# Delta-rule recurrence of a hybrid decoder layer: priority for its VectorE and ScalarE steps, and named places for its small products

## The chip, the cores and the metric

The kernel runs on one core of one Trainium2 chip. The metric is the device time of one execution in microseconds; the median of three runs of the kernel before is 2295.15 us (2294.39 to 2297.28).

## What is computed

Two layers of a parallel-branch decoder trunk with 512 tokens and a model width of 1024, in float32. Each layer normalises its input, projects it, runs three branches (a Mamba-2 scan, latent attention, a gated delta rule), merges them by sigmoid gates, projects the merge, and adds an MLP. The change lies in the gated delta rule. Cut to that, the reference is:

```python
def gated_delta_chunked(q, k, v, g, beta):      # L = 64 tokens a chunk
    ...
    a_mat = jnp.where(strict, einsum(kb, k) * decay, 0.0)
    rhs = concatenate([v * beta, kb * exp(g)])
    u, w = split(triangular_solve(a_mat + eye, rhs))
    qk = where(incl, einsum(q, k) * decay, 0.0)

    def step(state, inp):
        v_new = uc - wc @ state
        o = (qc * exp(gc)) @ state + ac @ v_new
        state = state * exp(g_last) + (kc * exp(g_last - gc)).T @ v_new
        return state, o

def gdn_mixer(...):
    ...
    o = rmsnorm(gated_delta_chunked(q, k, v, g, beta), norm_g) * silu(z)

mixed = g_ssd * (y_ssd @ w_ssd_out) + g_mla * (y_mla @ w_mla_out) + g_gdn * (y_gdn @ w_gdn_out)
```

## The kernel before, in words

**Dense products.** Each float32 operand is split into a rounded high part and the rest (`split_half`, L172 on ScalarE and L173 on VectorE, both with priority for weights), and a product is three matmuls of 128 x 128 by 512 (`mm3`, L200 to L202). `dense_F` (the weights stationary) forms two output tiles of 128 columns from eight k tiles: 48 matmuls, ordered by pairs of k tiles and within them by output tile `j`. It takes a `tag`; after the last matmul of k tile `kk` for output `j`, it calls `place((tag, kk, j), ...)`. The weights of a pair of k tiles need one of four buffers, and raw weights come through two. There are four PSUM banks for dense products (`acc`), three for small ones (`sm`), one for others (`yt`).

**The order.** The program is written tile by tile; a scheduler, run when the program is built, decides each engine's instruction order by priority and by its own model of durations, and adds semaphores. On the chip each engine runs its list in order. `tc.high_priority()` puts the instructions inside it ahead of others that are ready. `behind(key, ins)` asks that `ins` come after the matmul that `place` records under `key`, in TensorE's list alone: it adds no semaphore. Before the change it is used in the Mamba branch and in `gdn_matrix`.

**The delta rule.** Eight value heads are worked as two units (`gdn_unit`, `u` = 0 and 1) of four heads, two key heads each, in four steps `t` of 128 tokens. `gdn_matrix` and `gdn_inverse` have made the inverse `Y` of the triangular system ahead. A unit first does its dense products: the query tiles (`key_tiles`, tag `(ly, "k", 2u)`), the values (two `dense_F`), and the gate `z` (`silu_T`). Then come the four steps; the scheduler lays them among the dense products that follow in the program: those of unit 1 for unit 0, and the output projection's for unit 1 (`out_proj`: for each pair `dp` of output tiles a gate product, tag `(ly, 2, dp, "g")`, and a `y` product, tag `(ly, 2, dp, "y")`, whose k tiles 0 to 3 are unit 0's results and 4 to 7 unit 1's). One step holds:

- `pg` (L1039, TensorE): keys by queries; `gk` (L1041) and `pt_` (L1043) on VectorE mask and scale it; the decays `e` come by DMA.
- `pk` (L1048): keys by state; four VectorE instructions (L1050), one a head, subtract it from the values: `r`.
- `pw` (L1053): `Y` by `r`, one matmul a head, each seen in the trace as two instructions.
- `vn` (L1055, VectorE) and `vd` (four at L1060, ScalarE) scale `pw`.
- `pS` (L1063) and four VectorE instructions (L1069) make the next state. It closes the loop: the next step's `pk` waits for it.
- `po` (L1072) and, for t > 0, `pq` (L1077) give the output; ScalarE copies `po` (L1078), VectorE adds `pq` (L1080).
- The closing norm: squares (L1086, ScalarE), small VectorE instructions (L1090 to L1095) with a power on GpSimd in their midst (L278), and the gate, four at L1098.

After the four steps the gated tiles are transposed by columns `c` (L1103, four a column, in the one `yt` bank) and split into `yh` and `yl` (L273 on ScalarE, L274 on VectorE). The values' and keys' causal convolution (`gconv_silu`, L719 and three L723 a tile) has priority on both engines already.

Of the kernel before, what the change touches and what calls it, by code (L numbers as in the profile page):

```python
# [14 lines left out]
AF = mybir.ActivationFunctionType  # L15
# [5 lines left out]
P = 128  # L21
S = 512
T = S // P
# [32 lines left out]
def hybrid_kernel(ctx, tc, a, out, depth=2, taps=None):  # L56
# [4 lines left out]
    def mk(pl, shape, dt, tag, bufs=None):  # L61
        return pl.tile(shape, dt, tag=tag, name=f"{tag}_{next(uid)}", bufs=bufs)
# [120 lines left out]
    def weights(w2d, c0, n, K, hold=None, raw0=None):  # L183

        kt = min(1024 // n, K // P)
        step = 512 // n
        for k0 in range(0, K // P, kt):  # L190
            given = raw0 is not None and k0 == 0
            raw = raw0 if given else weights_raw(w2d, c0, n, k0, kt)
            for q in range(0, kt, step):
                hi, lo = split_half(raw[:, q * n : (q + step) * n], hold and hold[k0 + q], not given)
                v = lambda x: x.rearrange("p (k n) -> p k n", n=n)
                yield k0 + q, v(hi), v(lo)
# [37 lines left out]
    def tiles(n):  # L234
        return [slice(i, i + P) for i in range(0, n, P)]
# [147 lines left out]
    for ly in range(depth):  # L383
# [612 lines left out]
        def gdn_unit(u, kT, ork, cc, cd, Yt, yh, yl):  # L996
            hd0 = 16 + 4 * u
            qT = key_tiles(2 * u, between)
            pss = sm_bank()
            for i in range(2):  # L1000
                sq = mk(br, [P, S], F32, "ft4", 2)
                act.activation(sq, qT[i], AF.Square)
                for t in range(T):
                    pe.matmul(pss[:, i * T + t : i * T + t + 1], sq[:, t * P : (t + 1) * P], ones[:, 0:1], start=True, stop=True)
            ssq = mk(sp, [P, 2, T], F32, "gss", 2)
            dve.tensor_scalar(ssq.rearrange("p i t -> p (i t)"), pss[:, :8], 4.0 * EPS, None, ALU.add)
            rq = mk(sp, [P, 2, T], F32, "grq", 2)
            pool.tensor_tensor(rq.rearrange("p i t -> p (i t)"), ssq.rearrange("p i t -> p (i t)"), nhalf[:, :8], ALU.pow)
            ktok = [mk(br, [P, T, P], F32, "kt", 2) for i in range(2)]
            for i in range(2):  # L1010
                ps = sm_bank()
                for t in range(T):
                    pe.transpose(ps[:, t * P : (t + 1) * P], kT[i][:, t * P : (t + 1) * P], ident)
                act.copy(ktok[i].rearrange("p t n -> p (t n)"), ps)
            v = mk(br, [P, T, 512], F32, "tok", 5)
            gz = mk(br, [P, T, 512], F32, "tok", 5)
            for i in range(2):
                for j, pj in enumerate(dense_F(weights(w_in, O_GV + (4 * u + 2 * i) * P, 256, D), tiles(256), D, xh, xl)):
                    h = 2 * i + j
                    vf = mk(br, [P, S], F32, "ft4", 2)  # L1020
                    gconv_silu(pj, 8 + 4 * u + h, vf)
                    ps = sm_bank()
                    for t in range(T):
                        pe.transpose(ps[:, t * P : (t + 1) * P], vf[:, t * P : (t + 1) * P], ident)
                    dve.tensor_tensor(v[:, :, h * P : (h + 1) * P], ps.rearrange("p (t n) -> p t n", t=T),
                                      bc_last(ork[:, i, :], P), ALU.mult)
            silu_T(br, O_GZ + 512 * u, gz)

            hdec = lambda i, t, h: dec[:, i, t, hd0 + h : hd0 + h + 1]
            ss = mk(sp, [P, T, 4], F32, "gos", 2)  # L1030
            st = None
            for t in range(T):
                tok = slice(t * P, (t + 1) * P)
                Y = Yt[:, t]
                e = mk(br, [P, 4, P], F32, "eE", 4)
                sync.dma_start(e, d_e[u, t])
                pg = sm_bank()
                for i in range(2):
                    pe.matmul(pg[:, i * P : (i + 1) * P], kT[i][:, tok], qT[i][:, tok], start=True, stop=True)  # L1039
                gk = mk(br, [P, 2, P], F32, "gk", 2)  # L1040
                dve.tensor_tensor(gk, hv(pg)[:, 0:2], bc_mid(incl, 2), ALU.mult)  # L1041
                pt_ = e
                dve.tensor_tensor(prs(pt_), prs(e), bc_j(gk), ALU.mult)  # L1043
                r = v[:, t, :]
                if t > 0:
                    pk = sm_bank()
                    for i in range(2):
                        pe.matmul(pk[:, i * 256 : (i + 1) * 256], kT[i][:, tok], st[:, i * 256 : (i + 1) * 256], start=True, stop=True)  # L1048
                    for h in range(4):
                        dve.scalar_tensor_tensor(hv(r)[:, h], hv(pk)[:, h], ndec[:, t, 4 * u + h : 4 * u + h + 1], hv(r)[:, h], ALU.mult, ALU.add)  # L1050
                pw = sm_bank()
                for h in range(4):
                    pe.matmul(pw[:, h * P : (h + 1) * P], Y[:, h, :], r[:, h * P : (h + 1) * P], start=True, stop=True)  # L1053
                vn = mk(br, [P, 512], F32, "wk1")
                dve.tensor_tensor(hv(vn), hv(pw), bc_last(cc[:, t, :], P), ALU.mult)  # L1055
                sn = None
                if t < T - 1:
                    vd = mk(br, [P, 512], F32, "wk2")
                    for h in range(4):
                        act.activation(hv(vd)[:, h], hv(pw)[:, h], AF.Copy, scale=cd[:, t, h : h + 1])  # L1060
                    pS = sm_bank()
                    for i in range(2):
                        pe.matmul(pS[:, i * 256 : (i + 1) * 256], ktok[i][:, t, :], vd[:, i * 256 : (i + 1) * 256], start=True, stop=True)  # L1063
                    sn = mk(br, [P, 512], F32, "st", 2)
                    if t == 0:
                        act.copy(sn, pS)
                    else:
                        for h in range(4):
                            dve.scalar_tensor_tensor(hv(sn)[:, h], hv(st)[:, h], hdec(2, t, h), hv(pS)[:, h], ALU.mult, ALU.add)  # L1069
                po = sm_bank()  # L1070
                for h in range(4):
                    pe.matmul(po[:, h * P : (h + 1) * P], pt_[:, h, :], vn[:, h * P : (h + 1) * P], start=True, stop=True)  # L1072
                o = mk(br, [P, 512], F32, "wk3")
                if t > 0:
                    pq = sm_bank()
                    for i in range(2):
                        pe.matmul(pq[:, i * 256 : (i + 1) * 256], qT[i][:, tok], st[:, i * 256 : (i + 1) * 256], start=True, stop=True)  # L1077
                    act.copy(o, po)  # L1078
                    for h in range(4):
                        dve.scalar_tensor_tensor(hv(o)[:, h], hv(pq)[:, h], hdec(0, t, h), hv(o)[:, h], ALU.mult, ALU.add)  # L1080
                else:
                    act.copy(o, po)
                st = sn
                for h in range(4):
                    jk = mk(br, [P, P], F32, "gk", 2)
                    act.activation(jk, o[:, h * P : (h + 1) * P], AF.Square, accum_out=ss[:, t, h : h + 1])  # L1086

                rqt = mk(sp, [P, 4], F32, "grt", 2)
                for j in range(2):
                    dve.tensor_scalar(rqt.rearrange("p (i j) -> p i j", j=2)[:, :, j], rq[:, :, t], 128.0 ** -0.5, None, ALU.mult)  # L1090
                ms = mk(sp, [P, 4], F32, "gms", 2)
                dve.tensor_tensor(ms, ss[:, t, :], rqt, ALU.mult)
                dve.tensor_tensor(ms, ms, rqt, ALU.mult)
                rsq(ms, ms, 1.0 / 128, EPS)
                dve.scalar_tensor_tensor(ms, ms, 0.5, rqt, ALU.mult, ALU.mult)  # L1095
                for h in range(4):
                    gzh = hv(gz[:, t, :])[:, h]
                    dve.scalar_tensor_tensor(gzh, gzh, ms[:, h : h + 1], hv(o)[:, h], ALU.mult, ALU.mult)  # L1098
            for c in range(4):
                k = 4 * u + c  # L1100
                ps = y_bank()
                for t in range(T):
                    pe.transpose(ps[:, t * P : (t + 1) * P], gz[:, t, c * P : (c + 1) * P], ident)  # L1103
                split_gain(yh[k], yl[k], ps, col(g_gdn))
                tap(f"ygdn{k}", f32(yh[k]))

# [337 lines left out]
```

## Time and profile before

| | |
|---|---|
| median of 3 runs | 2295.15 us |
| profiled execution, its own time | 2296.46 us |
| its span | 2294.7 us |
| memory read and written over the span | 103 GB/s |
| dense matmul over a 512-wide tile, modelled duration | about 0.39 us |
| weight casts L172 over 512 columns | 536 from `wraw`, 620 ns each |
| weight rests L173 over 512 columns | 536 from `wraw`, 686 ns each |

The span is what the hardware profiler saw of the program between its first and last instruction; the profiled execution's own time is a little longer. Views give start and duration in microseconds, the engine, the source line, the operation, the tiles written and read, and how many like instructions follow each other; in brackets stands how long the engine had been idle and what ended the wait. PE is TensorE, PEld its weight load, DVE VectorE, ACT ScalarE, POOL GpSimd. Ends of matmuls are modelled, so what one costs in a stream is read from start to start. In the table of windows a row has the stretch and its length, then each engine's busy time and instructions (PE, PEld, DVE, ACT, POOL), the granted clock, the DMA share and GB/s. In the list of waits a row has the waiting line, what it waited for, the total in microseconds, the number of waits, and the longest.

### The profile page before, as it was taken

The page shows a single profiled execution, that of the slowest core. Times are in us where ns is not written, and L with a number is a line of the kernel's source. Part 1 is how long each engine was busy: PE and PEld are TensorE (multiplying, and loading weights), DVE is VectorE, ACT ScalarE, POOL GpSimd, SP SyncE. Part 2 cuts the span into 40 slices and gives each one's busy share as a digit, 9 for nine tenths or more (in the row PEclk, how much of TensorE's full clock was granted, in tenths as well). Part 3 has the DMA queues.
Part 4 walks back from the last instruction along what each step waited for, and adds up shares of the span by engine and source line. Part 5 has one row for each costly group of instructions (what it writes and reads, how often), then busy time and mean ns, then how long its engine had stood idle before and what let it go on. Part 6 is the DMA issues. An engine that isn't in the chain of part 4 may idle for free. (4 is left out here: it accounts for less than half of the span.)

```text
span 2294.7 us, 32300 instructions
## 1 busy us (share of the span) xinstructions
PE 2266.6 (99%) x11822; PEld 1863.0 (81%) x11822; DVE 1647.0 (72%) x3258; ACT 1205.9 (53%) x2508; POOL 59.5 (3%) x75
## 2 busy tenths in 40 slices
PE   9999999999999999999999999999999999999998
PEld 8888787888887888888888887878888877888886
DVE  7776567876666778767867775668757667778668
ACT  6766744333444465554657667443334435645545
POOL 0000000000000000000000000000000100000000
PEclk9999999999999999999999999999999999999999
DMA  4223634452224143233132236344422241432231
GB/s 144 81 74 101 193 101 120 126 151 74 79 69 167 64 147 110 92 107 106 52 100 78 77 103 202 92 120 141 127 81 76 65 166 55 165 106 100 89 110 47
DMA packets 220176, 244.23 MB, mean 106 GB/s; under 512 B 34272, under 2 KB 172528, under 8 KB 220016
## 3 DMA queue, kind: packets, MB, share of 16 engines
q1 hardware_dynamic: 220016, 242.16, 34.5%
q8 instruction: 93, 1.52, 0.3%
q14 instruction: 67, 0.55, 0.1%
HBM read 225.66 MB, written 11.74 MB: 103 GB/s over the span
## 5 line engine op out<-in xcount | busy, mean ns | idle before, releaser
L172 ACT CAST whi<-wraw 128x512 fp32r<-128x512 f32 (+1 forms) x536 | 330.6, 620 | 531.9 <-PE acc L201 367.2
L173 DVE TENSOR_TENSOR wlo<-wraw,whi 128x512 fp32r<-128x512 f32 (+1 forms) x536 | 365.3, 686 | 339.5 <-ACT whi L172 334.0
L200 PE MATMUL acc<-xh,whi 128*128 128x512 f32 (+1 forms) x1344 | 523.1, 390 | 0.0
L202 PE MATMUL acc<-xh,wlo 128*128 128x512 f32 (+1 forms) x1344 | 522.2, 389 | 0.0
L201 PE MATMUL acc<-xl,whi 128*128 128x512 f32 (+1 forms) x1344 | 521.6, 388 | 0.0
L202 PEld LDWEIGHTS acc<-xh,wlo 128*128 128x128 f32 x1344 | 252.7, 188 | 47.8
L201 PEld LDWEIGHTS acc<-xl,whi 128*128 128x128 f32 x1344 | 252.9, 188 | 47.5 <-DVE xl L274 0.7
L200 PEld LDWEIGHTS acc<-xh,whi 128*128 128x128 f32 x1344 | 252.6, 188 | 47.8 <-ACT xh L273 0.4
L172 ACT CAST whi<-wr 128x512 fp32r<-128x512 f32 x168 | 104.6, 623 | 107.4 <-PE acc L201 47.4
L201 PE MATMUL acc<-yl,whi 128*128 128x512 f32 x384 | 151.6, 395 | 0.0
L200 PE MATMUL acc<-yh,whi 128*128 128x512 f32 x384 | 150.5, 395 | 0.0
L202 PE MATMUL acc<-yh,wlo 128*128 128x512 f32 x384 | 150.5, 392 | 0.0
L173 DVE TENSOR_TENSOR wlo<-wr,whi 128x512 fp32r<-128x512 f32 x168 | 113.4, 688 | 35.4 <-ACT whi L172 34.7
L723 DVE SCALAR_TENSOR_TENSOR ckl<-acc,pc,ckl 128x511 f32<-128x511 f32 (+2 forms) x168 | 120.3, 744 | 18.0 <-ACT ckl L719 10.8
L200 PEld LDWEIGHTS acc<-yh,whi 128*128 128x128 f32 x384 | 71.7, 188 | 16.2 <-ACT yh L273 1.7
L202 PEld LDWEIGHTS acc<-yh,wlo 128*128 128x128 f32 x384 | 72.2, 188 | 14.3
L201 PEld LDWEIGHTS acc<-yl,whi 128*128 128x128 f32 x384 | 72.2, 188 | 13.9
L201 PE MATMUL acc<-wlo,xh 128*128 128x512 f32 (+1 forms) x208 | 79.9, 384 | 0.0
L202 PE MATMUL acc<-whi,xl 128*128 128x512 f32 (+1 forms) x208 | 79.6, 384 | 0.0
L200 PE MATMUL acc<-whi,xh 128*128 128x512 f32 (+1 forms) x208 | 79.5, 384 | 0.0
L1184 DVE TENSOR_TENSOR h<-h,acc 128x512 f32<-128x512 f32 x120 | 77.1, 681 | 0.1
L486 ACT ACTIVATE eE<-eE,cum 128x128 f32<-128x128 f32 x192 | 62.9, 393 | 27.0 <-DMA eE<-d_c 25.1
(462 smaller groups left out, 4554.4 us busy)
## 6 DMA issues: line engine op xcount, KB each, us to landing
wraw<-in_w_in_dram SPq DMA_DIRECT2D x144, 512.0 KB, 3.6
wraw<-in_w_up_dram SPq DMA_DIRECT2D x64, 512.0 KB, 3.6
wr<-in_w_down_dram SPq DMA_DIRECT2D x32, 1024.0 KB, 5.1
eE<-d_c SPq DMA_DIRECT2D x48, 256.0 KB, 4.5
wraw<-in_w_mla_out_dram SPq DMA_DIRECT2D x16, 512.0 KB, 3.5
eE<-d_e SPq DMA_DIRECT2D x32, 256.0 KB, 3.0
wraw<-in_w_ssd_out_dram SPq DMA_DIRECT2D x16, 512.0 KB, 3.4
wraw<-in_w_gdn_out_dram SPq DMA_DIRECT2D x16, 512.0 KB, 3.4
```

What stands on the lines that cost most here:

```text
L172: act.copy(hi, raw)
L173: dve.tensor_tensor(lo, raw, f32(hi), ALU.subtract)
L200: pe.matmul(o, ah, bh, start=start, stop=False, skip_group_check=more)
L201: pe.matmul(o, ah, bl, start=False, stop=False, skip_group_check=more)
L202: return pe.matmul(o, al, bh, start=False, stop=stop, skip_group_check=more)
L486: act.activation(o[:, i], o[:, i], AF.Relu, scale=-1.0, bias=cum[:, t, h0 + i : h0 + i + 1])
L723: dve.scalar_tensor_tensor(acc[:, d:], ps[:, : S - d], taps_[3 - d], acc[:, d:], ALU.mult, ALU.add)
L1184: dve.tensor_tensor(hs_, hs_, ps[t], op)
```

## The change

It tags the value product; it names three dense products `seq` that follow each unit; it puts L1050, L1055, L1060 and L1069 under priority; and it asks that `pg` (from t = 2), `pw` (from t = 1), `po` (t = 3) and the transposes of the first column come behind named matmuls of those products. No instruction is added or taken away, and no arithmetic changes.

```diff
-                for j, pj in enumerate(dense_F(weights(w_in, O_GV + (4 * u + 2 * i) * P, 256, D), tiles(256), D, xh, xl)):
+                for j, pj in enumerate(dense_F(weights(w_in, O_GV + (4 * u + 2 * i) * P, 256, D), tiles(256), D, xh, xl, tag=(ly, "v", 4 * u + 2 * i))):
...
             ss = mk(sp, [P, T, 4], F32, "gos", 2)
+            g_, y_ = ((ly, 2, i // 2, "gy"[i % 2]) for i in range(2))
+            seq = [(ly, "k", 2), (ly, "v", 4), (ly, "v", 6)] if u == 0 else [g_, y_, (ly, 2, 1, "g")]
+            pw_place = (seq[0], 3, 0), (seq[0], 5, 1), (seq[1], 1, 0)
+            pg_place = (seq[0], 5, 0), (seq[0], 7, 1)
+            end_place = (seq[2], 1, 0) if u == 0 else (seq[2], 5, 0)
             st = None
             for t in range(T):
...
                 for i in range(2):
-                    pe.matmul(pg[...], kT[i][:, tok], qT[i][:, tok], start=True, stop=True)
+                    x = pe.matmul(pg[...], kT[i][:, tok], qT[i][:, tok], start=True, stop=True)
+                    if t > 1:
+                        behind(pg_place[t - 2], x)
...
                     for h in range(4):
-                        dve.scalar_tensor_tensor(hv(r)[:, h], hv(pk)[:, h], ndec[...], hv(r)[:, h], ALU.mult, ALU.add)
+                        with tc.high_priority():
+                            dve.scalar_tensor_tensor(hv(r)[:, h], hv(pk)[:, h], ndec[...], hv(r)[:, h], ALU.mult, ALU.add)
                 pw = sm_bank()
                 for h in range(4):
-                    pe.matmul(pw[...], Y[:, h, :], r[...], start=True, stop=True)
+                    x = pe.matmul(pw[...], Y[:, h, :], r[...], start=True, stop=True)
+                    if t > 0:
+                        behind(pw_place[t - 1], x)
                 vn = mk(br, [P, 512], F32, "wk1")
-                dve.tensor_tensor(hv(vn), hv(pw), bc_last(cc[:, t, :], P), ALU.mult)
+                with tc.high_priority():
+                    dve.tensor_tensor(hv(vn), hv(pw), bc_last(cc[:, t, :], P), ALU.mult)
...
-                        act.activation(hv(vd)[:, h], hv(pw)[:, h], AF.Copy, scale=cd[:, t, h : h + 1])
+                        with tc.high_priority():
+                            act.activation(hv(vd)[:, h], hv(pw)[:, h], AF.Copy, scale=cd[:, t, h : h + 1])
...
-                            dve.scalar_tensor_tensor(hv(sn)[:, h], hv(st)[:, h], hdec(2, t, h), hv(pS)[:, h], ALU.mult, ALU.add)
+                            with tc.high_priority():
+                                dve.scalar_tensor_tensor(hv(sn)[:, h], hv(st)[:, h], hdec(2, t, h), hv(pS)[:, h], ALU.mult, ALU.add)
                 po = sm_bank()
                 for h in range(4):
-                    pe.matmul(po[...], pt_[:, h, :], vn[...], start=True, stop=True)
+                    x = pe.matmul(po[...], pt_[:, h, :], vn[...], start=True, stop=True)
+                    if t == T - 1:
+                        behind((seq[1], 1, 1), x)
...
                 for t in range(T):
-                    pe.transpose(ps[:, t * P : (t + 1) * P], gz[:, t, c * P : (c + 1) * P], ident)
+                    x = pe.transpose(ps[:, t * P : (t + 1) * P], gz[:, t, c * P : (c + 1) * P], ident)
+                    if c == 0:
+                        behind(end_place, x)
```

More of the change, by code (lines that the diff above doesn't have):

```diff
@@ L1038, in gdn_unit @@
                 for i in range(2):
-                    pe.matmul(pg[:, i * P : (i + 1) * P], kT[i][:, tok], qT[i][:, tok], start=True, stop=True)
+                    x = pe.matmul(pg[:, i * P : (i + 1) * P], kT[i][:, tok], qT[i][:, tok], start=True, stop=True)
+                    if t > 1:
+                        behind(pg_place[t - 2], x)
                 gk = mk(br, [P, 2, P], F32, "gk", 2)
@@ L1049, in gdn_unit @@
                     for h in range(4):
-                        dve.scalar_tensor_tensor(hv(r)[:, h], hv(pk)[:, h], ndec[:, t, 4 * u + h : 4 * u + h + 1], hv(r)[:, h], ALU.mult, ALU.add)
+                        with tc.high_priority():
+                            dve.scalar_tensor_tensor(hv(r)[:, h], hv(pk)[:, h], ndec[:, t, 4 * u + h : 4 * u + h + 1], hv(r)[:, h], ALU.mult, ALU.add)
                 pw = sm_bank()
                 for h in range(4):
-                    pe.matmul(pw[:, h * P : (h + 1) * P], Y[:, h, :], r[:, h * P : (h + 1) * P], start=True, stop=True)
+                    x = pe.matmul(pw[:, h * P : (h + 1) * P], Y[:, h, :], r[:, h * P : (h + 1) * P], start=True, stop=True)
+                    if t > 0:
+                        behind(pw_place[t - 1], x)
                 vn = mk(br, [P, 512], F32, "wk1")
-                dve.tensor_tensor(hv(vn), hv(pw), bc_last(cc[:, t, :], P), ALU.mult)
+                with tc.high_priority():
+                    dve.tensor_tensor(hv(vn), hv(pw), bc_last(cc[:, t, :], P), ALU.mult)
                 sn = None
@@ L1068, in gdn_unit @@
                         for h in range(4):
-                            dve.scalar_tensor_tensor(hv(sn)[:, h], hv(st)[:, h], hdec(2, t, h), hv(pS)[:, h], ALU.mult, ALU.add)
+                            with tc.high_priority():
+                                dve.scalar_tensor_tensor(hv(sn)[:, h], hv(st)[:, h], hdec(2, t, h), hv(pS)[:, h], ALU.mult, ALU.add)
                 po = sm_bank()
                 for h in range(4):
-                    pe.matmul(po[:, h * P : (h + 1) * P], pt_[:, h, :], vn[:, h * P : (h + 1) * P], start=True, stop=True)
+                    x = pe.matmul(po[:, h * P : (h + 1) * P], pt_[:, h, :], vn[:, h * P : (h + 1) * P], start=True, stop=True)
+                    if t == T - 1:
+                        behind((seq[1], 1, 1), x)
                 o = mk(br, [P, 512], F32, "wk3")
```

## The prediction

> **What bounds the kernel.** I read the page first: the engine totals and the row of the granted clock.
>
> ```profile
> span 2294.7 us, 32300 instructions
> PE 2266.6 (99%) x11822; PEld 1863.0 (81%) x11822; DVE 1647.0 (72%) x3258; ACT 1205.9 (53%) x2508; POOL 59.5 (3%) x75
> PEclk9999999999999999999999999999999999999999
> ```
>
> TensorE is busy for 99% of the span at the full granted clock, so the time is the sum of what it is given to do plus its few pauses, 28.1 us in all (2294.7 - 2266.6). The change adds and removes no instruction. It can win only pauses, or the cost of switching between dense and small products. So the next view is the list of TensorE's waits, and after it the busy time in the four stretches in which the delta rule's recurrence runs (two units in each of two layers).
>
> ```profile
> PE sm L1053 <- DVE tok L1050: 3.5, 8, 0.5
> PE yt L1103 <- DVE tok L1098: 2.9, 4, 1.0
> ```
> ```profile
> 584.25:636.71 52.46, 51.56 (x276) 42.40 (x274) 38.32 (x101) 23.23 (x65) 3.90 (x3) 1.00 0.28 81
> 664.56:715.00 50.44, 48.14 (x254) 38.76 (x253) 31.62 (x96) 21.10 (x66) 4.40 (x4) 1.00 0.18 53
> 1722.10:1774.60 52.50, 51.59 (x276) 42.42 (x274) 38.37 (x101) 23.27 (x65) 3.91 (x3) 1.00 0.29 81
> 1802.40:1853.00 50.60, 48.30 (x255) 38.87 (x254) 31.61 (x96) 21.14 (x67) 4.40 (x4) 1.00 0.17 53
> ```
>
> The lines that the change touches, L1053 (`pw`) and L1103 (the closing transposes), lead that list: 12 pauses, 6.4 us. The layers repeat each other (52.46 and 52.50 us for unit 0, 50.44 and 50.60 us for unit 1), so I work one layer and double it. VectorE has 38.32 us of work in 52.46 us, so it has room: it is late by its order, not by its load.
>
> **What one pause costs.** The ends of products are modelled, so a pause is priced from starts, in TensorE's timeline of unit 0.
>
> ```profile
> 584.69 1.06 PE L1053 MATMUL sm<-tok,tok 128*128 128x128 f32 x8
> ...
> 586.05 0.39 PE L202 MATMUL acc<-xh,wlo 128*128 128x512 f32 x1
> ...
> 588.32 0.39 PE L200 MATMUL acc<-xh,whi 128*128 128x512 f32 x1
> ...
> 591.79 0.59 PE L202 MATMUL acc<-xh,wlo 128*128 128x512 f32 x1
> ...
> 594.59 0.38 PE L1053 MATMUL sm<-tok,tok 128*128 128x128 f32 x2
> 594.73 0.47 PE L202 MATMUL acc<-xh,wlo 128*128 128x512 f32 x1
> 595.61 0.49 PE L1053 MATMUL sm<-tok,tok 128*128 128x128 f32 x2 [0.41 <-DVE tok L1050]
> 595.94 0.27 PE L1103 MATMUL yt<-ct,tok 128*128 128x128 f32 x1
> ...
> 598.56 1.19 PE L1063 MATMUL sm<-wk,kt 128*128 128x256 f32 x4
> ...
> 602.46 0.58 PE L202 MATMUL acc<-xh,wlo 128*128 128x512 f32 x1
> ...
> 603.11 0.40 PE L201 MATMUL acc<-xl,whi 128*128 128x512 f32 x1
> 603.34 0.40 PE L1053 MATMUL sm<-tok,tok 128*128 128x128 f32 x2
> ...
> 604.74 0.38 PE L1053 MATMUL sm<-tok,tok 128*128 128x128 f32 x2
> ...
> 606.35 0.40 PE L201 MATMUL acc<-xl,whi 128*128 128x512 f32 x1
> 607.24 0.33 PE L1103 MATMUL yt<-ct,tok 128*128 128x128 f32 x1 [0.49 <-DVE tok L1098]
> ```
> ```profile
> 698.51 0.49 PE L1053 MATMUL sm<-tok,tok 128*128 128x128 f32 x2 [0.40 <-DVE tok L1050]
> ...
> 706.22 0.39 PE L202 MATMUL acc<-xh,wlo 128*128 128x512 f32 x1
> 707.56 0.33 PE L1103 MATMUL yt<-ct,tok 128*128 128x128 f32 x1 [0.95 <-DVE tok L1098]
> ```
>
> Ten dense products start between 586.05 and 588.32 us: 0.227 us each. (One matmul of L1053 shows as two instructions, a pair.) At 594.73 the next start comes 0.88 us later: 0.65 lost. The pair that was waited for then takes 0.33 us to the next start, and the pair at 594.59 took 0.14: 0.19 more. So an L1053 pause costs 0.84 us, and the eight cost 6.7. A pause before L1103 costs (607.24 - 606.35) - 0.227 = 0.66 in unit 0 and (707.56 - 706.22) - 0.227 = 1.11 in unit 1; two layers 3.5. **Pauses at stake: 10.2 us.**
>
> **Switching.** From 603.11 to 604.74 lie six dense products and one pair: 1.63 - 1.36 = 0.27 for the pair. In the group of eight at 584.69, which with two dense products reaches to 586.05, a pair takes (1.36 - 0.45) / 4 = 0.227. Joining saves 0.045 per pair; with some 11 pairs that stand apart in each of four units it is **2.0 us** (0 if the new order splits other groups instead).
>
> **Part 1, priority on VectorE and ScalarE.** L1050 (`r`), L1055 (`vn`), L1060 (`vd`) and L1069 (the state) go ahead of whatever else is ready. VectorE's timeline shows what it heals:
>
> ```profile
> 592.18 0.35 DVE L1050 SCALAR_TENSOR_TENSOR tok<-sm,ndec,tok 128x128 f32<-128x128 f32 x1 [2.46 <-PE sm L1048]
> ...
> 595.13 0.16 DVE L1095 SCALAR_TENSOR_TENSOR gms<-gms,grt 128x4 f32<-128x4 f32 x1 [0.87 <-POOL gms L278]
> 595.21 0.34 DVE L1050 SCALAR_TENSOR_TENSOR tok<-sm,ndec,tok 128x128 f32<-128x128 f32 x1
> 595.48 0.87 DVE L1098 SCALAR_TENSOR_TENSOR tok<-tok,gms,wk 128x128 f32<-128x128 f32 x3
> ...
> 597.12 0.68 DVE L1055 TENSOR_TENSOR wk<-sm,gcc 128x512 f32<-128x512 f32 x1
> ...
> 601.59 1.12 DVE L1080 SCALAR_TENSOR_TENSOR wk<-sm,dec,wk 128x128 f32<-128x128 f32 x4 [0.69 <-ACT wk L1078]
> ```
>
> The four L1050 of one step lie from 592.18 to 595.55 with the closing norm's L1095 between them, which sat 0.87 us for GpSimd's power and held the last L1050 behind it. Back to back, at 1.12 / 4 = 0.28 each by the like L1080, they end by 593.4. L1055 then waited again behind L1098, to 597.12.
>
> **Part 2, the places.** A place is a lower bound in TensorE's own order, without a semaphore. For the step t=1 the group stands behind k tile 3 of the named dense product, that is its 21st matmul of 48; counted in the same timeline, its first pair now goes after the 17th, its last after the 24th. When L1048 has been issued (the dense product at 591.79 is the 15th), seven dense matmuls come before the group, about 1.8 us: 593.6, against data at 593.4. I cost t=1 at nothing; were it late by one 0.87 wait, 1.06 us with the restart, in each of four units.
>
> For t=2 the place is 15 dense matmuls later: 15 x 0.227 = 3.4, and the small products between, 598.56 to 602.46, 3.9: 7.3 us from group to group. The chain from the end of one `pw` (595.94) to the start of the next (603.34) took 7.4 us, of which L1055 waited about 0.9 behind L1098: 6.5 undelayed. Slack 0.8, or none where L1055 falls behind L1095 again. For t=3 there are 21 dense matmuls, 4.8 + 3.9 = 8.7 us: over a microsecond of slack either way. So I leave a new pause at the four groups of t=2, each priced by the nearest row, 0.87 and the restart of 0.19: **4.2 us** lost. Bounds: 0, and 12 groups x 1.06 = 12.7.
>
> The transposes of column 0 no longer stand singly. In unit 0 they come behind the third dense product's 9th matmul, the 105th dense matmul from the group at 584.69, and t=3's group stands at the 57th: 48 matmuls, 10.9 us, against 8.7 us that the closing chain needed in unit 1 (its last pair starts at 698.51, its L1103 at 707.56: 9.1 us less that pair's 0.33). In unit 1 the place is behind 48 + 24 + 33 = 105 dense matmuls against 96 now, 2.0 us later, with 15 dense ones left behind it. Four transposes and a split pair by column take about 2.2 us, 1.8 of them eight dense products, and the matmuls that need column 0 come first; I cost it at nothing, bound 1 us a layer. `pg` of t=2 and t=3 is held as well; its readers L1041 and L1043 thereby leave the crowded stretch. No DMA is issued elsewhere; the load of `e` keeps its four buffers.
>
> **What is pushed back.** Weight splits and `gconv_silu`'s taps stand behind the recurrence's bursts on VectorE and ScalarE.
>
> ```profile
> L173 DVE TENSOR_TENSOR wlo<-wraw,whi 128x512 fp32r<-128x512 f32 x30 | 20.6, 688 | 10.7 <-ACT whi L172 10.7
> L172 ACT CAST whi<-wraw 128x512 fp32r<-128x512 f32 x30 | 18.6, 621 | 27.6 <-PE acc L201 19.7 <-PE acc L202 7.8
> L278 POOL TENSOR_TENSOR gms<-gms,nhalf 128x4 f32<-128x4 f32 x8 | 9.3, 1164 | 148.8 <-DVE gms L277 128.9 <-DVE gss L1006 19.9
> ```
>
> The casts wait for TensorE to free a buffer: the four buffers are full, and each feeds 12 matmuls, 2.7 us, so a burst of 1.12 us stays covered. Without that cover (unit 1, where the second half of the `y` weights holds two of four) the margin is 2.7 - 0.62 - 0.69 = 1.4 us, still above one burst. Nothing is added.
>
> **Sum:** -10.2 - 2.0 + 4.2 = -8.0 us. The profiled execution took 2296.46 us, 1.8 outside its span and 1.3 above the median of 2295.15. Taken off the median: **2287.1 us**. Its own range: all pauses gone, -12.2, 2282.9; the residual doubled, -3.8, 2291.3.
>
> **Rivals.** First, the pauses move but stay. What speaks for it: L278 takes 1.16 us and VectorE waited 0.87 at L1095; one queue serves both, and L1055 and L1069 can meet the same wait. If each of the 12 groups is late by that, 12.7 us return: -12.2 + 12.7, **2295.7**. Against it: the slack of t=3 above. The Trainium skill, "TensorE: Matmul & The Clock Gate", opening table, calls VectorE's queue strictly first-in first-out, and in Part 3, "The mechanism", says that matmuls keep their order in start and end. The trace agrees with both: L1050 stood behind L1095 for 0.87 us, and no dense product passed the pair at 595.61. By those rules a place is as bad as its latest input, which is this rival.
>
> Second, slower: the small products' PSUM banks, three of them.
>
> ```profile
> 600.72 0.59 ACT L1078 COPY wk<-sm 128x512 f32<-128x512 f32 x1 [1.23 <-PE sm L1072]
> ```
>
> L1078 and L1080 empty the banks of `po` and `pq` and get no priority; passed by the recurrence, they hold two banks while `pg`, `pk`, `pw` and `pS` want them. If each group waits for one such emptying, 0.59 + 1.12 + 0.19 = 1.9 us, the 12 cost 22.8: 22.8 - 12.2 = +10.6, **2305.8**. It decides from 12.2 / 12 = 1.02 us a group. Against it: TensorE shows no such wait now, and VectorE has 14 us free in 52.
>
> Third, the change doesn't do what it says: for t=2 and t=3 the old pairs already lie behind the places, so only priority moves them. Should priority change little, t=1 (4 x 0.84) and the transposes (3.5) are won, 6.9 us: **2288.2**.
>
> **Chances.** Forecast 0.62, first rival 0.18, second 0.14, third 0.06. A difference under 0.2% (4.6 us) can't be told from none. Faster is forecast and third rival, 0.68; same the first, 0.18; slower the second, 0.14. Both signs hold weight, so the range runs from 2281.5 (all won, and a microsecond more from groups that happen to join) to 2297 (the first rival and a little over); it leaves out the slower case.
>
> **What would show it.** Right: L1053 runs as groups of eight for every t, the wait for L1050 falls from 3.5 us to about 1, the wait of L1103 vanishes, the four L1050 stand together on VectorE, and the unit 1 stretches shrink by about 3 us, unit 0's by about 1. Wrong: a wait of L1053, L1048 or L1063 over 1 us at each step, a wait of dense products for L172 or L173, a wait for L1080, or pauses elsewhere that give it back.

## The result, and the profile after

| | before | after |
|---|---|---|
| median, 22 runs each, in turns | 2295.82 us | 2291.78 us |
| ratio, 95% interval | | 0.9982 [0.9976, 0.9988] |
| profiled execution, its own time | 2296.46 us | 2290.89 us |
| its span | 2294.7 us | 2289.1 us |

The kernel became 4.0 us faster by the medians, half of the 8.0 us forecast. The change is real, since the interval excludes 1, and it is just under the 0.2% that the prediction took as what can be told from nothing. One of the 22 runs of before took 4575.38 us; the ratio is over the others. The two profiled executions lie 5.6 us apart, 1.6 more than the medians, so the two spans are not used below for the size of the effect.

The added lines shift the numbers. What was L1050 (`r`) is L1058, L1053 (`pw`) is L1061, L1055 (`vn`) is L1066, L1060 (`vd`) is L1072, L1063 (`pS`) is L1075, L1090 is L1105, L1095 is L1110, L1098 is L1113, L1103 (the transposes) is L1118. The page of the kernel after:

```profile
span 2289.1 us, 32304 instructions
PE 2264.0 (99%) x11822; PEld 1866.7 (82%) x11822; DVE 1647.4 (72%) x3258; ACT 1202.8 (53%) x2508; POOL 58.7 (3%) x75
PEclk9999999999999999999999999999999999999999
```

TensorE does the same 11822 matmuls at the same clock, so the difference can only be pauses and switching. The list of TensorE's waits after (the waiting line, what it waited for, total, number, longest):

```profile
PE sm L1075 <- ACT wk L1072: 3.1, 4, 0.8
...
PE sm L1024 <- DVE ft L282: 1.0, 2, 0.5
...
PE yt L1118 <- DVE tok L1113: 0.7, 2, 0.3
```

The eight waits of `pw` (3.5 us) are gone, and of the transposes' 2.9 us 0.7 are left. Two waits are new: `pS` for `vd`, four times, and L1024 (the transposes of unit 1's values) for the convolution, twice.

To compare kernels stage by stage, the same dense matmul is found in both, by counting the starts of L200 to L202. Unit 0's stretch runs from the 2011th to the 2303rd such start, unit 1's from there to the 2441st (first layer). The windows between those starts show stretch and length, then the engines' busy times. Before:

```profile
572.01:664.10 92.09, 91.19 (x465) 75.07 (x464) 62.00 (x148) 41.34 (x100) 6.58 (x5) 1.00 0.29 85
664.10:718.70 54.60, 52.30 (x271) 41.99 (x270) 34.01 (x99) 23.50 (x69) 4.40 (x4) 1.00 0.17 49
```

After:

```profile
571.39:663.95 92.56, 90.95 (x465) 75.73 (x464) 62.15 (x148) 41.49 (x100) 6.10 (x5) 1.00 0.29 85
663.95:715.98 52.03, 51.25 (x272) 42.62 (x270) 33.96 (x98) 22.91 (x68) 4.46 (x4) 1.00 0.20 58
```

Unit 1 went from 54.60 to 52.03 us, 2.57 less; unit 0 from 92.09 to 92.56, 0.47 **more**. The second layer, by the 6341st, 6639th and 6781st start, gives -2.59 and +0.47. The four together are -4.2 us, which is what the medians show (-4.0). So the question is why unit 0 lost.

**The new wait of `pS`.** TensorE's timeline after, around step t=1 of unit 0, and the same place at t=2:

```profile
592.29 1.05 PE L1061 MATMUL sm<-tok,tok 128*128 128x128 f32 x8
...
594.55 0.39 PE L200 MATMUL acc<-xh,whi 128*128 128x512 f32 x1
595.72 0.70 PE L1075 MATMUL sm<-wk,kt 128*128 128x256 f32 x2 [0.78 <-ACT wk L1072]
...
604.59 0.40 PE L200 MATMUL acc<-xh,whi 128*128 128x512 f32 x1
604.93 0.70 PE L1075 MATMUL sm<-wk,kt 128*128 128x256 f32 x2
```

`pw` now runs as a group of eight, with no wait. From the last dense product to `pS` it is 595.72 - 594.55 = 1.17 us at t=1 and 604.93 - 604.59 = 0.34 at t=2: 0.83 lost. VectorE's timeline of the same moment shows why:

```profile
590.18 1.13 DVE L1058 SCALAR_TENSOR_TENSOR tok<-sm,ndec,tok 128x128 f32<-128x128 f32 x4 [2.98 <-PE sm L1055]
...
592.65 0.69 DVE L1050 TENSOR_TENSOR eE<-eE,gk 128x512 f32<-128x512 f32 x1
594.25 0.16 DVE L1110 SCALAR_TENSOR_TENSOR gms<-gms,grt 128x4 f32<-128x4 f32 x1 [0.90 <-POOL gms L278]
594.32 0.68 DVE L1066 TENSOR_TENSOR wk<-sm,gcc 128x512 f32<-128x512 f32 x1
```

The four L1058 stand together, 1.13 us, as forecast. But L1110, the closing norm's step after GpSimd's power, is ahead of L1066 in VectorE's order. `pw`, begun at 592.29 and eight products long, was done when VectorE stood still from about 593.3 to 594.2, and L1066 could have run in that hole. It starts at 594.32, `vd` follows, and `pS` is late. The wait of 0.9 us that held `r` before now holds `vn`.

**The wait of L1024.** VectorE after, and TensorE after, later in unit 0:

```profile
623.10 0.17 DVE L1006 TENSOR_SCALAR gss<-sm 128x8 f32<-128x8 f32 x1 [0.78 <-PE sm L1004]
625.02 0.24 DVE L1105 TENSOR_SCALAR grt<-grq 128x2 f32<-128x2 f32 x2 [1.75 <-POOL grq L1008]
625.16 1.12 DVE L1095 SCALAR_TENSOR_TENSOR wk<-sm,dec,wk 128x128 f32<-128x128 f32 x4
627.14 0.75 DVE L723 SCALAR_TENSOR_TENSOR ckl<-acc,pc,ckl 128x511 f32<-128x511 f32 x1 [0.86 <-ACT ckl L719]
```
```profile
632.25 0.39 PE L200 MATMUL acc<-xh,whi 128*128 128x512 f32 x1
633.15 0.66 PE L1024 MATMUL sm<-ct,ft 128*128 128x128 f32 x4 [0.51 <-DVE ft L282]
...
634.73 0.40 PE L200 MATMUL acc<-xh,whi 128*128 128x512 f32 x1
```

L1105 belongs to unit 1's step 0 and needs another power, L1008, over the norms of unit 1's queries. It is in VectorE's order directly behind the instruction that feeds that power (L1006), so VectorE waits 1.75 us, and L1095, the squares and the convolution's taps come late behind it. Before, the list of VectorE's waits had this wait only twice, after it has it four times; the list of before, then of after:

```profile
DVE grt L1090 <- POOL grq L1008: 3.5, 2, 1.8
```
```profile
DVE grt L1105 <- POOL grq L1008: 7.0, 4, 1.8
```

### The profile page after: what moved, and what is told of

It is laid out like the page before. It is cut to its first block, busy times and chain, and to the rows that moved or that the text cites. A ratio compares the mean times of both kernels' runs of the same rounds, so it can differ in the third digit from the quotient of the medians.

```text
span 2289.1 us, 32304 instructions
## 1 busy us (share of the span) xinstructions
PE 2264.0 (99%) x11822; PEld 1866.7 (82%) x11822; DVE 1647.4 (72%) x3258; ACT 1202.8 (53%) x2508; POOL 58.7 (3%) x75
## 4 chain that ended last, share of the span: by engine, by line
PE 91%; DVE 3%; ACT 2%; POOL 1%; DMA 1%; issue 0%; DVEq 0%; POOLq 0%; ACTq 0%; SPq 0%
PE acc L200 23%; PE acc L202 23%; PE acc L201 23%; PE sm L200 3%; PE sm L202 3%; PE sm L201 3%; DVE wlo L173 1%; PE sm L784 1%; PE sm L682 1%; PE sm L1085 1%; PE sm L1075 1%; PE yt L698 1%; ACT whi L172 1%; PE sm L662 1%; PE sm L659 0%
## 5 line engine op out<-in xcount | busy, mean ns | idle before, releaser
L200 PE MATMUL acc<-xh,whi 128*128 128x512 f32 (+1 forms) x1344 | 524.5, 391 | 0.0
L202 PE MATMUL acc<-xh,wlo 128*128 128x512 f32 (+1 forms) x1344 | 519.8, 387 | 0.0
L202 PEld LDWEIGHTS acc<-xh,wlo 128*128 128x128 f32 x1344 | 252.5, 188 | 48.8
L200 PEld LDWEIGHTS acc<-xh,whi 128*128 128x128 f32 x1344 | 252.5, 188 | 48.1 <-ACT xh L273 0.4
L200 PE MATMUL acc<-yh,whi 128*128 128x512 f32 x384 | 151.5, 398 | 0.0
L202 PE MATMUL acc<-yh,wlo 128*128 128x512 f32 x384 | 150.4, 392 | 0.0
L723 DVE SCALAR_TENSOR_TENSOR ckl<-acc,pc,ckl 128x511 f32<-128x511 f32 (+2 forms) x168 | 121.1, 744 | 20.7 <-ACT ckl L719 13.0
L200 PEld LDWEIGHTS acc<-yh,whi 128*128 128x128 f32 x384 | 71.5, 188 | 16.7 <-ACT yh L273 2.3
L202 PEld LDWEIGHTS acc<-yh,wlo 128*128 128x128 f32 x384 | 72.2, 188 | 14.6
L200 PE MATMUL acc<-whi,xh 128*128 128x512 f32 (+1 forms) x208 | 79.9, 386 | 0.0
L202 PE MATMUL acc<-whi,xl 128*128 128x512 f32 (+1 forms) x208 | 78.7, 381 | 0.0
```

Of the source, the lines that this page charges most:

```text
L200: pe.matmul(o, ah, bh, start=start, stop=False, skip_group_check=more)
L202: return pe.matmul(o, al, bh, start=False, stop=stop, skip_group_check=more)
L723: dve.scalar_tensor_tensor(acc[:, d:], ps[:, : S - d], taps_[3 - d], acc[:, d:], ALU.mult, ALU.add)
```

## The experiments

The theory (A): the places and the priority do remove the pauses, and the lost half goes to powers on GpSimd, for which VectorE stands in its queue ahead of the recurrence. The rivals: the groups themselves cost time (held PSUM banks, groups that come late); or only one of the two parts does anything. All ratios are to the kernel before on the same chip. Every kernel below computes all of the reference.

**1. Priority alone.** The four calls of `behind` that the change adds are taken out:

```diff
-                    if t > 1:
-                        behind(pg_place[t - 2], x)
...
-                    if c == 0:
-                        behind(end_place, x)
```

> The priority of the four recurrence steps alone, without any named place. Theory A (VectorE's order makes the pauses: a step of the recurrence stands behind a norm step that waits for GpSimd): the eight pauses of pw on L1050 (6.7 us) go, the pauses of the closing transposes (3.5 us) stay, and the wait of pS on vd that the changed kernel shows (3.1 us, four times) stays; about 2 to 4 us faster than before. Theory B (the grouping on TensorE makes the gain, priority is idle): within 1 us of before, with pw's pauses in place.

Measured 1.0015 [1.0006, 1.0024]: slower, a clear miss of the 2 to 4 us gain expected. Its list of TensorE's waits says where it went:

```profile
PE yt L1112 <- DVE tok L1107: 6.0, 4, 2.0
...
PE sm L1044 <- DVE st L1078: 1.3, 4, 0.3
...
PE sm L1044 <- ACT wk L1087: 0.8, 4, 0.2
```

The recurrence is prompt, but the closing work is now what is passed over, while its transposes keep their early places on TensorE: 6.0 us of waits, against 2.9 before. Priority on two engines without places on the third only moves the lateness. The two waits of L1044 are `pg`, which reads keys and queries alone, neither the state of L1078 nor the copied `po` of L1087. So it can only wait for the PSUM banks that these two empty, 2.1 us in all: the second rival's wait, in small.

In unit 1 the two layers of this kernel differ, +1.32 and -0.17 us against before (the table below), with the same waits of TensorE in both, the longest 2.0 us. In the first layer the granted clock was low for some 3 us behind that longest wait; the window, with the clock in the third column from the end:

```profile
702.00:705.00 3.00, 3.00 (x10) 2.40 (x9) 1.30 (x2) 0.80 (x2) 0.00 (x0) 0.50 0.00 0
```

Dense products start 0.43 us apart there instead of 0.23. In the second layer the clock stayed at 1.00 behind the same wait. So about 1.5 of the stretches' 2.5 us of loss is a low clock in one layer of the profiled execution; whether the other executions had it, and what set it off, is not shown.

**2. Places alone.**

```diff
-                        with tc.high_priority():
+                        with nullcontext():
```

(four times)

> The named places alone, without priority. Theory A: pw's groups stand together but meet their last L1050 late, so TensorE still pauses on L1050 (3 us or more in all); only the transposes' pauses go in unit 1; 1 to 4 us faster than before. Theory B: the whole gain of the change, 4 us, and pauses of pw gone.

Measured 0.9995 [0.9987, 1.0004], at the low end of the 1 to 4 us expected and not told from nothing. TensorE waits eight times before `pw`, as in the kernel before:

```profile
PE sm L1061 <- DVE tok L1058: 3.6, 8, 0.5
```

So neither half gains anything measurable alone, and together they gain 0.18%.

**3. The closing norm's step behind the next `vn`.** An order within VectorE's own list, without a semaphore; `place` names an instruction, `behind` puts another after it:

```diff
-                    dve.tensor_tensor(hv(vn), hv(pw), bc_last(cc[:, t, :], P), ALU.mult)
+                    place((ly, "vn", u, t), dve.tensor_tensor(hv(vn), hv(pw), bc_last(cc[:, t, :], P), ALU.mult))
...
-                dve.scalar_tensor_tensor(ms, ms, 0.5, rqt, ALU.mult, ALU.mult)
+                x = dve.scalar_tensor_tensor(ms, ms, 0.5, rqt, ALU.mult, ALU.mult)
+                if t < T - 1:
+                    behind((ly, "vn", u, t + 1), x)
```

> The changed kernel, with the norm step that waits for GpSimd's power ordered behind the next step's vn on VectorE. Theory A: that wait (0.90 us on VectorE ahead of L1066) is what makes pS late at t=1, so the four waits of pS on vd (3.1 us, with the restart about 3.5) vanish: about 3 us faster than the changed kernel, ratio to before 0.9968 or so. Rival: vd is late by ScalarE's own queue (a weight cast between its parts), then the wait stays and the time is that of the changed kernel, 0.998.

Measured 0.9964 [0.9952, 0.9977]. VectorE of this kernel, at the same step:

```profile
597.61 0.69 DVE L1050 TENSOR_TENSOR eE<-eE,gk 128x512 f32<-128x512 f32 x1
598.33 0.69 DVE L1066 TENSOR_TENSOR wk<-sm,gcc 128x512 f32<-128x512 f32 x1
599.20 0.16 DVE L1110 SCALAR_TENSOR_TENSOR gms<-gms,grt 128x4 f32<-128x4 f32 x1 [0.18 <-POOL gms L278]
```

L1066 follows 0.72 us behind L1050's start instead of 1.67 (594.32 - 592.65), L1110's wait shrinks from 0.90 to 0.18, and the waits of `pS` are gone from TensorE's list. Each of the four stretches lost 0.90 to 0.96 us against after, 3.7 together. (The profiled execution of this kernel was the slowest of its five, 2292.62 us against a median of 2287.05; most of that lies ahead of the first stretch, which starts 5.0 us later than after's.) The first half of theory A stands.

**4. The change in unit 1 alone** (every new line conditioned on `u`, as `if u and t > 1:`).

> The whole change in unit 1 alone, unit 0 as before. Theory A: the gain is unit 1's (2.6 us a layer by the starts of the dense products), unit 0 gives back 0.4 to 0.5 us a layer: about 1 us faster than the changed kernel, ratio to before 0.9977. Rival (both units gain alike): half the gain, ratio 0.9990.

Measured 0.9978 [0.9969, 0.9987], as expected, though the runs alone cannot tell it from the whole change. The stretches of unit 1 are as in the change (-2.58 and -2.61), those of unit 0 as before (-0.09, +0.01). The change as made gains everything in unit 1, and pays for it in unit 0.

**5. The order of experiment 3 on the kernel before**, without priority and places: the same two edits.

> The kernel before with one order alone: the norm step that waits for GpSimd's power comes behind the next step's vn on VectorE; no priority and no place. Theory A (that wait, 0.87 us ahead of the last L1050, makes most of pw's pauses): pw's waits on L1050 fall from 3.5 us to under 1.5; the transposes' pauses stay or grow, since the norm comes later; 1 to 6 us faster than before. Rival (priority is what heals pw): pw's waits stay at 3 us or more and the time is that of before.

Measured 0.9987 [0.9978, 0.9996], a gain of 3 us, within what was expected. The pauses of `pw` vanish altogether, and the transposes' remain, 3.6 us:

```profile
PE yt L1105 <- DVE tok L1100: 3.6, 4, 0.9
```

One order edge on VectorE does what the change does for `pw`: the cause of those eight pauses was L1095 in VectorE's queue, and neither a want of priority nor of places.

**6. Priority with the places of `po` and the transposes**, and **7. priority with the places of `pg` and `pw`** (of the four calls of `behind`, two are taken out in each).

> Priority and the closing places (po of the last step, transposes of column 0), without the places of pg and pw. Theory A (priority alone lost because the early single transposes then met the norm late, 6.0 us of waits): those waits go, and the time is that of the changed kernel within 2 us, ratio 0.9975 to 0.999. Rival (the groups of pw are needed): no faster than priority alone, 1.001 or more.

> Priority and the places of pg and pw, without the closing places. Theory A: the transposes' waits stay (4 to 6 us), so nothing is gained: ratio 0.999 to 1.001. Rival (grouping the steps' products is the gain): ratio 0.998.

Measured 0.9990 [0.9981, 0.9999] and 0.9987 [0.9978, 0.9995]: each half of the places gains 2 to 3 us with priority. For experiment 7 that is a miss: nothing was expected to be gained. In the first the transposes no longer wait, but L1024 does (2.4 us) and `pg` does (2.0, and 0.8 for the copy of `po`); in the second the transposes wait 5.2 us, and `pg` not at all. The two lists of TensorE's waits:

```profile
PE sm L1024 <- DVE ft L282: 2.4, 2, 1.2
...
PE sm L1044 <- DVE st L1078: 2.0, 4, 0.5
```
```profile
PE yt L1116 <- DVE tok L1111: 5.2, 6, 1.0
```

Waits of `pg` for the emptying of the banks show in the three kernels that have priority without the places of `pg` and `pw`: 2.1 us in experiment 1, 2.8 in 6, 2.2 in 9. They show neither in before nor in the change, nor in any kernel that keeps those places or the old priorities. So the rival that the groups wait for banks is out for the change as made, and the places of `pg` and `pw` are what keeps it out.

**8. Both powers out of the way**: experiment 3, and L1105 behind its own step's `vn`:

```diff
-                    dve.tensor_scalar(rqt.rearrange("p (i j) -> p i j", j=2)[:, :, j], rq[:, :, t], 128.0 ** -0.5, None, ALU.mult)
+                    behind((ly, "vn", u, t), dve.tensor_scalar(rqt.rearrange("p (i j) -> p i j", j=2)[:, :, j], rq[:, :, t], 128.0 ** -0.5, None, ALU.mult))
```

> The kernel of e3 with a second order on VectorE: L1105, which for unit 1 waits for another power of GpSimd (VectorE idle 1.75 us in unit 0's crowded stretch), comes behind its own step's vn; TensorE's order is the same as in e3. Theory A: unit 0's pauses at the values' and closing transposes (about 1.5 us a layer) shrink by 1 us or more a layer: 2 to 3 us faster than e3, ratio to before about 0.9953. Rival (those pauses come from the convolution's load on VectorE): the time of e3, 0.9964.

Measured 0.9962 [0.9950, 0.9975], median 2286.43 us, the fastest of all. The runs cannot tell it from experiment 3, and so cannot show the 2 to 3 us expected. The traces can, since TensorE's order is the same in both: unit 0's stretch lost 0.93 and 0.97 us more, 1.9 together, unit 1's 0.02 at most. Its windows, then VectorE and TensorE at the place shown of after:

```profile
572.36:663.04 90.68, 90.39 (x466) 75.83 (x465) 62.00 (x148) 41.34 (x100) 6.10 (x5) 1.00 0.30 86
663.04:714.13 51.09, 51.09 (x272) 42.63 (x270) 34.05 (x102) 22.91 (x68) 4.46 (x4) 1.00 0.20 59
```
```profile
623.12 0.17 DVE L1006 TENSOR_SCALAR gss<-sm 128x8 f32<-128x8 f32 x1 [0.78 <-PE sm L1004]
623.21 1.12 DVE L1095 SCALAR_TENSOR_TENSOR wk<-sm,dec,wk 128x128 f32<-128x128 f32 x4
626.22 0.75 DVE L723 SCALAR_TENSOR_TENSOR ckl<-acc,pc,ckl 128x511 f32<-128x511 f32 x1 [1.89 <-ACT ckl L719]
```
```profile
632.26 0.39 PE L200 MATMUL acc<-xh,whi 128*128 128x512 f32 x1
632.50 0.60 PE L1024 MATMUL sm<-ct,ft 128*128 128x128 f32 x4
...
633.84 0.40 PE L200 MATMUL acc<-xh,whi 128*128 128x512 f32 x1
```

L1006 is at the same time in both executions (623.10 and 623.12); with no wait behind it the tap L723 comes 0.92 us earlier, and the two groups of L1024, with the dense products around them, take 633.84 - 632.26 = 1.58 us instead of 634.73 - 632.25 = 2.48. That is the 0.9 us per layer. In unit 1, TensorE is busy for all of the 51.09 us.

**9. Priority with both orders, without places**, and **10. places with both orders, without priority.**

> e8 without the named places: priority and the two orders on VectorE. Theory A (once no recurrence step stands behind a power, what is left of TensorE's pauses is the single closing transposes, which run early and meet the norm late): waits of the transposes of 3 us or more, ratio to before between 0.998 and 1.000. Rival (places add nothing once the orders are right): the time of e8, 0.996.

> e8 without priority: the places and the two orders on VectorE. Theory A (the orders, not priority, take the power out of the recurrence's way): pw's waits on L1050 under 1.5 us in all, unit 1's stretch at least 2 us shorter than before, ratio 0.9965 to 0.998. Rival (priority is needed as well): waits of pw on L1050 of 3 us and ratio 0.999 or more.

Measured 1.0005 [0.9995, 1.0014], just outside the 0.998 to 1.000 expected, and 0.9965 [0.9953, 0.9978], as expected. Without places the transposes still wait, 5.5 us in the list of TensorE's waits:

```profile
PE yt L1114 <- DVE tok L1109: 5.5, 4, 1.8
```

With places and orders but no priority, the four L1058 are spread out again, yet nothing holds the last; the windows and VectorE's timeline:

```profile
572.46:663.42 90.96, 90.58 (x465) 75.64 (x464) 61.40 (x148) 41.22 (x100) 6.04 (x5) 1.00 0.30 86
663.42:714.80 51.38, 51.38 (x272) 42.43 (x270) 33.74 (x102) 23.04 (x68) 4.03 (x4) 1.00 0.20 58
```
```profile
594.36 0.60 DVE L1058 SCALAR_TENSOR_TENSOR tok<-sm,ndec,tok 128x128 f32<-128x128 f32 x2
595.65 0.69 DVE L1066 TENSOR_TENSOR wk<-sm,gcc 128x512 f32<-128x512 f32 x1 [0.68 <-PE sm L1061]
...
596.85 0.15 DVE L1110 SCALAR_TENSOR_TENSOR gms<-gms,grt 128x4 f32<-128x4 f32 x1
```

The stretches are 0.28 and 0.29 us longer than with priority (90.96 - 90.68, 51.38 - 51.09), so given the two orders priority is worth about 1.1 us in four stretches. So the rival of the one part holds under that condition alone: with the powers out of the way, the places carry nearly all.

All stretches against before, in microseconds (first layer, second layer), with the ratio of the runs:

```
                                unit 0          unit 1          sum     runs
after                         +0.47  +0.47    -2.57  -2.59     -4.2   0.9982
1  priority alone             +0.64  +0.69    +1.32  -0.17     +2.5   1.0015
2  places alone               +0.07  +0.15    -0.64  -0.67     -1.1   0.9995
3  after, norm behind vn      -0.49  -0.43    -3.49  -3.53     -7.9   0.9964
4  after in unit 1 alone      -0.09  +0.01    -2.58  -2.61     -5.3   0.9978
5  before, norm behind vn     -0.25  -0.17    -1.67  -1.68     -3.8   0.9987
6  priority, po and end       +0.63  +0.61    -2.44  -2.45     -3.7   0.9990
7  priority, pg and pw        -0.67  -0.56    -1.16  -1.15     -3.5   0.9987
8  3, and L1105 behind vn     -1.42  -1.40    -3.51  -3.52     -9.9   0.9962
9  8 without places           +0.57  +0.66    -0.27  -0.26     +0.7   1.0005
10 8 without priority         -1.13  -1.09    -3.23  -3.27     -8.7   0.9965
```

A ratio of 0.001 is 2.3 us, and every sum agrees with its runs to within about 1.4 us (for priority alone with the low clock counted in): what is at stake lies in these four stretches.

## Why the prediction was right in sign and twice too large

**Pauses at stake, -10.2 us: near, by experiment 10.** It removes the pauses by places and orders and gains 8.7 us; of the recurrence's waits on TensorE it keeps only the transposes' 0.7 us, two pauses, or about 1.1 with the restart that the prediction priced at 0.19 each. Together that is 9.8. Hardly any of it is switching, since the small products form 49 runs a layer before and 48 in experiment 10. Experiment 5 speaks for a lower price: it removes the eight pauses of `pw` and adds 0.7 us to the transposes' waits, which by the prediction's prices is 6.7 - 0.7 = 6.0 us, and its stretches gain 3.8. That difference stays open.

**Switching, -2.0 us: right in sign, half the size.** Between experiments 10 and 8 the groups join (in the first layer from 29 runs of small products to 20 in unit 0's stretch, from 19 to 14 in unit 1's), and the gain is 1.1 us. The step that failed is "some 11 pairs that stand apart in each of four units": 14 runs a layer joined, 28 in two layers and not 44 (30 from before to after); at 0.045 each that would be 1.3.

**The new pause, +4.2 us: right cause and size, wrong place.** The prediction left four groups late behind a wait of VectorE like L1095's, 1.06 us each. Measured by taking it away (experiment 3): 0.90 to 0.96 us each, 3.7 in all. But it forecast `pw` of t=2 as the late one. That group has no wait in the trace; the late one is `pS` of t=1, through `vn` and `vd`. Two steps failed.

The prediction worked out when the named products would come, and asked of the instructions that feed them only; `pS` has no place of its own, but follows seven dense products behind `pw` (593.10 to 594.55 us at t=1), and its feeder stands in the same queue. The Trainium skill, "TensorE: Matmul & The Clock Gate", opening table, names VectorE's queue as strictly first-in first-out; the trace agrees, with 0.90 us in which L1066 was ready and stood behind L1110.

It also miscounted the places. Within a pair of k tiles `dense_F` finishes one output tile before the other, so the last matmul of k tile 3 for the first output is the 18th of 48, not the 21st; the third place is the 54th, not the 57th, and that of the transposes the 102nd, not the 105th. In unit 1 of after, the groups of `pw` start 18, 36 and 54 dense matmuls behind the group of t=0. The second and third, and what follows the second:

```profile
683.08 1.06 PE L1061 MATMUL sm<-tok,tok 128*128 128x128 f32 x8
683.89 0.48 PE L200 MATMUL acc<-xh,whi 128*128 128x512 f32 x1
...
692.27 1.05 PE L1061 MATMUL sm<-tok,tok 128*128 128x128 f32 x8
```

From the end of one group to the next it is 692.27 - 683.89 = 8.4 us where nothing waits, and not 7.3. Against the 6.5 us that the prediction gave the chain, `pw` of t=2 had 1.9 us of slack instead of 0.8, and the wait that it was charged would have been covered. So the right sum is partly luck: the same wait of VectorE fell on four other groups. For t=1 the right count would have made the group about 0.5 us late by the prediction's own figures (three dense products less than its 593.6, against 593.4); it was not late, since `pk` starts at 589.11 us instead of 591.07, and `r` is done by 591.31.

**The missing term, +1.9 us.** In the part on what is pushed back, the prediction asked whether the taps of `gconv_silu` and the weights' splits would be late behind bursts of the recurrence, and answered "Nothing is added." It quoted the row of GpSimd's powers, 19.9 us of whose idle time L1006 ended, and did not ask what else on VectorE waits for a power. Once the recurrence is prompt, unit 1's L1105 is scheduled early, into the stretch where unit 0's last step and unit 1's convolution meet, and its 1.75 us delay the taps. That is most of why unit 0, forecast at -1 us, got +0.47; unit 1, without this term, was forecast at -3 and got -2.6.

The sum by what was measured: -9.85 (nearly all pauses gone and the grouping, experiment 8) + 3.7 + 1.9 = -4.2 us, against -4.0 by the medians. It comes out at the stretches of after by its making, since the two terms are differences between the same kernels; what it shows is how the forecast's terms compare.

**The signs that were named.** `pw` in groups of eight at every t: yes. The wait for `r` down to about 1 us: to none. The transposes' wait gone: 0.7 of 2.9 left. The four L1058 together: yes. Of the signs against, "a wait of L1053, L1048 or L1063 over 1 us at each step" came in a smaller form: L1063 (now L1075), 0.8 us, at one step of each unit; "pauses elsewhere that give it back" came in L1024.

**The rivals.** The first (pauses move but stay) was half true: 5.6 of 9.85 us came back, through just the mechanism it named, GpSimd's power in VectorE's queue, at four groups instead of twelve and at one more place. The second (PSUM banks) did not show in the change; its wait exists, 2.1 to 2.8 us in the three kernels with priority and without the places of `pg` and `pw`. The third (priority does nothing) is refuted as it was put: without priority the change gains nothing that can be measured (experiment 2, 0.9995), where the rival gave 2288.2 us. Yet that need of priority is mostly a need to have `r` ahead of L1110, as experiments 5 and 10 show.

**What stays open.** Why the transposes wait 6.0 us under priority alone was read from the trace and not taken apart further, nor was the low clock behind one of these waits. The pause of about 0.3 us of the last transpose of column 0 in unit 0 is left in experiment 8 too; only in experiment 6 does no transpose wait. The 1.6 us by which the two profiled executions lie further apart than the medians were not traced to a place.

## What to carry to other kernels

When TensorE is full, look for the instruction that stands at the head of another engine's queue waiting for a slow helper (here a power on GpSimd, for which VectorE waited 0.9 and 1.75 us), and order it behind the work that the critical loop needs; that edge alone took away the pauses of `pw`, though not those of the transposes. In this change priority and places need each other: priority without places left the closing transposes waiting and lost 0.15%, places without priority gained nothing measurable. With the two orders on VectorE, places without priority gained 0.35%. Count a named place in the order in which the loop really runs. After grouping a step's products, check the feeder of each group that follows, not only of those that got a place, and what work of the next stage the scheduler will now pull forward.

## What the runs showed of the hardware

A power over 128x4 elements on GpSimd took 1.115 us on average and over 128x8 1.64 us, while VectorE's L1066 over 128x512 takes 0.69 us on average. The groups by line of the kernel after, and an instance in its GpSimd timeline:

```profile
L278 POOL TENSOR_TENSOR gms<-gms,nhalf 128x4 f32<-128x4 f32 x16 | 17.8, 1115 | 279.7 <-DVE gms L277 279.7
```
```profile
623.35 1.64 POOL L1008 TENSOR_TENSOR grq<-gss,nhalf 128x8 f32<-128x8 f32 x1 [2.91 <-DVE gss L1006]
```

GpSimd is busy for 3% of the span, and putting the two readers of its powers behind other work on VectorE was worth 3.7 + 1.9 = 5.6 us of it. Switching between dense and small products on TensorE costs little: 1.1 us for 28 runs joined, about 0.04 us each. In experiment 1 the granted clock fell to 0.50 for some 3 us behind a 2.0 us pause of TensorE in one layer, and stayed at 1.00 behind the like pause in the other.
